# The second MLP product turned round: activations as the stationary operand, weights as 512 moving columns

## The chip, the cores and the metric

The kernel runs on one core of one Trainium2 chip. The metric is the device time of one execution in microseconds (us). The kernel before is given by the median of three runs; the profile is of one further execution.

## What is computed

One decoder layer with a convolution mixer, for 256 tokens (`T`) and 2048 channels (`D`), all in 32-bit floats. Cut to what matters:

```
mod = silu(c) @ mod_w + mod_b                  # six rows of 2048: sh1 sc1 g1 sh2 sc2 g2
h = rms_norm(x) * (1 + sc1) + sh1
y = conv_mixer(h)                              # product 2048 -> 4096, gate, causal conv, layer norm, product 2048 -> 2048
x = x + (1 + g1) * y
h = rms_norm(x) * (1 + sc2) + sh2
u = square(relu(h @ mlp_w1))                   # 2048 -> 8192
x = x + (1 + g2) * (u @ mlp_w2)                # 8192 -> 2048: the second MLP product
```

## The kernel before

**Layout.** Activations lie by channels: a tile is 128 channels by 256 tokens, and the residual `xs` is [128, 16, 256], 16 such tiles. All products before the change take a 128x128 block of weights as the stationary operand of TensorE and stream tokens as moving columns.

**Splitting into two parts.** A float is split into a high part in a shorter format (float32r) and a low part, the rest. `split_w` does it for a weight tile (1 MB, [128, 16, 128]) in two halves: ScalarE writes `hi` (L200), VectorE writes `lo` (L201, by subtraction; on GpSimd for a few tiles). There are six `hi` and six `lo` buffers of half a tile. `split_act` does the same for activations: the tile has 512 columns, 256 tokens of the high part and then 256 of the low part (ScalarE L208, VectorE L209).

**One job.** `mm` (L212 to L227) computes 128 output channels from 16 blocks of the contraction: per block one pass with `hi` stationary and all 512 columns moving (L223) and one with `lo` stationary and the 256 high columns (L224). A job does two such groups of 128 channels (c = 0, 1), into one PSUM tile `mm` of 128x2x512; there are two of these. `evac` adds the two halves: ScalarE copies one (L423), VectorE adds (L424). The out stage and the very last job use the `merged` form, three passes of 256 columns into the same columns (L219 to L221).

**Jobs in a row.** `jobs` lists 16 "in" jobs, 8 "out" jobs, and then for each of four quarters of the 8192 hidden channels 8 jobs ("up", q, i) and 8 jobs ("down", q, i). An up job ends with relu, square and `split_act` into `u2[i]`; a down job reads `u2` and adds its result, times the gate column of g2, into `xs` (L891). In the last quarter each down job sends its part of `xs` to the output (L895).

**Loads.** Every weight tile comes by one DMA of 1 MB on SyncE's queue (`top_up`, L180) into one of five `raw` buffers, in the order of the list `order`: for each job the two tiles of the next job, then the tiles named in `after[job]`. A load waits in the queue until its buffer is free.

**The modulation.** Rows of `mod` that are needed late are computed beside the jobs. The 16 tiles of g2 are "columns": `mod_col` multiplies a 1 MB tile of `mod_w` by a broadcast of silu(c) (`cb`) on VectorE with a running sum (L299), which yields one column of 128 values. `LATE_UP` and `LATE_DOWN` say how many of the 16 follow each job of the first quarter; `after[job]` holds them.

**Order on the engines.** A scheduler sets each engine's order once, at build time, from priorities and its own estimate of durations. `urgent()` raises a priority, `tc.issue_after` pins one instruction behind another. At run time an engine takes its instructions strictly in that order.

Of the kernel before, what the change touches and what calls it, by code (L numbers as in the profile page):

```python
# [14 lines left out]
P = 128  # L15
# [41 lines left out]
K_OUTER = [("out", 0), ("up", 0, 1), ("up", 0, 2)]  # L57
SIDE = 14
POOLED = [("out", 0), ("out", 1), ("up", 0, 1), ("up", 0, 2)]
LATE_UP = [0, 0, 1, 1, 1, 1, 2, 2]  # L60
LATE_DOWN = [1] * 8


@with_exitstack
def conv_block(ctx: ExitStack, tc: tile.TileContext, x, vec, dwq, c_row, mod_r, mod_c, w_first, w_in, w_out, w1, w2, out):
# [2 lines left out]
    const = ctx.enter_context(tc.tile_pool(name="const", bufs=1))  # L68
    wts = ctx.enter_context(tc.tile_pool(name="wts", bufs=1))
    acts = ctx.enter_context(tc.tile_pool(name="acts", bufs=1))  # L70
    tmp = ctx.enter_context(tc.tile_pool(name="tmp", bufs=2))
    ps = ctx.enter_context(tc.tile_pool(name="ps", bufs=2, space=PSUM))

# [62 lines left out]
    def source(key):  # L136
        kind = key[0]
        if kind == "mod":
            return mod_r[ROWS.index(key[1]), key[2]]
        if kind == "col":  # L140
            return mod_c[COLS.index(key[1])]
        if kind == "first":
            return w_first[key[1]]
        if kind == "in":
            return w_in[key[1] + key[2] * KT]
        if kind == "out":
            return w_out[2 * key[1] + key[2]]
        if kind == "up":
            return w1[key[1] * KT + 2 * key[2] + key[3]]
        if kind == "down":  # L150
            return w2[2 * key[2] + key[3], key[1]]
        if kind == "x":
            return x
        return vec[:, soon:]
# [56 lines left out]
    def mm(p, c, key, acts_of, ks=range(KT), merged=False):  # L211
        halves = parts[key]  # L212
        for k in ks:
            hi, lo = halves[k // HALF]
            m = acts_of[k // 2][:, k % 2, :]
            if merged:
                out_p, begin, end = p[:, c, 0:T], k == 0, k == KT - 1
                w = hi[:, k % HALF, :]
                nc.tensor.matmul(out_p, w, m[:, 0:T], start=begin, stop=False)  # L219
                nc.tensor.matmul(out_p, w, m[:, T : 2 * T], start=False, stop=False)  # L220
                state["mm_end"] = nc.tensor.matmul(out_p, lo[:, k % HALF, :], m[:, 0:T], start=False, stop=end)  # L221
                continue
            nc.tensor.matmul(p[:, c, :], hi[:, k % HALF, :], m, start=(k == 0), stop=(k == KT - 1))  # L223
            state["mm_end"] = nc.tensor.matmul(  # L224
                p[:, c, T : 2 * T], lo[:, k % HALF, :], m[:, 0:T], start=False, stop=(k == KT - 1),
                skip_group_check=True,
            )  # L227

    row_ps = []
    pending = []  # L230
# [153 lines left out]
    for job in jobs:  # L384
        n = quota.get(job, 0)
        after[job], late = late[:n], late[n:]
        if job[0] in ("up", "down") and job[1] == 0:
            n = (LATE_UP if job[0] == "up" else LATE_DOWN)[job[2]]
            after[job], last = last[:n], last[n:]
    assert not late and not last  # L390

# [315 lines left out]
    for n, job in enumerate(jobs):  # L707
# [8 lines left out]
        if n == KT - 1:  # L716
            for key in parts_early:
                split_w(key, nc.gpsimd)
        p = ps.tile([P, 2, 2 * T], F32, name="mm", bufs=2)
        kind, i = job[0], job[-1]  # L720
        plain = kind == "up" and job[1] == 0 and i < UNSCALED
        if job == ("up", 0, 0):
            mm(p, 0, job + (0,), xa, range(SIDE))
            for at in range(2 * UNSCALED):
                shift_row(at, shown.pop(("up", 0, at // 2, at % 2)))
            fold_shift()
            mm(p, 0, job + (0,), xa, range(SIDE, KT))
            mm(p, 1, job + (1,), xa)
        elif job in K_OUTER:
            for k2 in range(HALF):  # L730
                for c in range(2):
                    mm(p, c, job + (c,), xa if plain else hl, range(2 * k2, 2 * k2 + 2), kind == "out")
        elif kind == "in":
            rows = list(after[job]) if i < KT - 1 else []
            for c in range(2) if i < KT - 1 else (1, 0):
                for ks in (range(HALF), range(HALF, KT)):
                    mm(p, c, job + (c,), hl, ks, i == KT - 1)
                    with tc.issue_after(state["mm_end"].ins):
                        mods(rows[:1])
                    del rows[:1]  # L740
        else:
            for c in range(2):
                mm(p, c, job + (c,), u2 if kind == "down" else hl, merged=kind == "out" or n == len(jobs) - 1)
        mod_finish()
        if kind == "in":
            with urgent():
# [118 lines left out]
        elif kind == "up":  # L865
            if job[1:] == (0, 0):
                for k2 in range(HALF):
                    modulate(k2, scaled(k2, r2), SH2, SC2, ps_two())
            with urgent() if plain else ExitStack():
                t2 = evac(p)  # L870
                a = two()
                if plain:
                    nc.vector.tensor_tensor(t2, t2, spread(r2), op=ALU.mult)
                    for c in range(2):
                        at = 2 * i + c
                        nc.scalar.activation(t2[:, c, :], t2[:, c, :], AF.Relu, bias=shc[:, at : at + 1])
                    nc.vector.tensor_tensor(a, t2, t2, op=ALU.mult)
                else:
                    nc.scalar.activation(t2, t2, AF.Relu)
                    nc.scalar.activation(a, t2, AF.Square)  # L880
            u2[i] = mp.tile([P, 2, 2 * T], F32R, name="u2", bufs=HALF)
            split_act(u2[i], a)
            mods(after[job])
        else:
            mods(after[job])
            halves = [slice(0, 1), slice(1, 2)] if n == len(jobs) - 1 else [slice(0, 2)]
            for cs in halves:
                t2 = evac(p, cs) if n < len(jobs) - 1 else p[:, cs, 0:T]
                for c in range(cs.start, cs.stop):
                    xk = pair_of(xs, i)[:, c, :]  # L890
                    nc.vector.scalar_tensor_tensor(  # L891
                        xk, t2[:, c - cs.start, :], mcol(G2, 2 * i + c), xk, op0=ALU.mult, op1=ALU.add
                    )
# [54 lines left out]
```

## Time and profile before

| what | value |
|---|---|
| median of 3 runs | 1124.28 us (1123.37 to 1127.79) |
| profiled execution, its own time | 1122.33 us |
| span of the profiled execution | 1120.5 us |
| TensorE busy | 98% of the span |
| VectorE, ScalarE, GpSimd busy | 69%, 52%, 15% |
| mean granted TensorE clock | 0.997 |
| data read from HBM | 290.14 MB, 261 GB/s over the span |

The profile is of one core. Times are in us from the span's start; "mean" columns and pieces marked so are in ns. A busy share is an average over stages. In the timeline a line gives the start, the duration, engine, source line and operation with "output<-inputs" and, in brackets, how long the engine was idle before and what ended that. Matmuls are pipelined: the distance from start to start, not the duration shown, is what one costs in a stream.

### The profile page before, as it was taken

To read this page: it belongs to the slowest core of one execution; us is meant where nothing else is said; L and a number is where in the kernel's file an instruction comes from. 1 tells how busy PE (TensorE), PEld (TensorE's weight loads), DVE (VectorE), ACT (ScalarE), POOL (GpSimd) and SP (SyncE) were. 2 spreads that over 40 slices of the span, in tenths; PEclk is the share of its full clock that TensorE was granted. 3 is DMA by queue.
4 is the path that set the end of the run, shared out by engine and by line. 5 is a ranking of instruction groups with operands and counts; after the bars stand their busy time and mean duration, and the time that the engine had idled before them with its cause. 6 is when DMAs were issued, how large, how long until landed. Compare 5 with 4: busy or idle time off the path is not lost.

```text
span 1120.5 us, 17425 instructions
## 1 busy us (share of the span) xinstructions
PE 1098.4 (98%) x7088; PEld 946.6 (84%) x7088; DVE 768.0 (69%) x1025; ACT 582.0 (52%) x806; POOL 166.6 (15%) x103
## 2 busy tenths in 40 slices
PE   6999999999999999999999999999999999999998
PEld 4888776766699998888888888888888888888888
DVE  3988689987489989887765555555555665555653
ACT  5222395664675587554445554444655444555441
POOL 0000086467533262000000000000000000000000
PEclk8999999999999999999999999999999999999999
DMA  9999979888599977888775555555554655555640
GB/s 384 420 421 420 418 307 346 349 322 318 207 390 350 371 283 276 290 350 299 273 259 192 190 193 194 193 191 193 189 190 165 211 188 188 188 188 188 209 139 29
DMA packets 41553, 293.35 MB, mean 262 GB/s; under 512 B 4609, under 2 KB 5121, under 8 KB 6401
## 3 DMA queue, kind: packets, MB, share of 16 engines
q1 hardware_dynamic: 41328, 292.17, 70.4%
q8 instruction: 55, 0.90, 0.3%
q14 instruction: 24, 0.20, 0.0%
q10 hardware_dynamic: 146, 0.08, 0.0%
HBM read 290.14 MB, written 2.10 MB: 261 GB/s over the span
## 4 chain that ended last, share of the span: by engine, by line
PE 86%; DMA 6%; DVE 6%; ACT 1%; issue 0%; POOL 0%; DVEq 0%; ACTq 0%; POOLq 0%
PE mm L223 45%; PE mm L224 24%; DMA raw<-mod_c 4%; PE mm L220 3%; DVE raw L299 3%; PE mm L219 3%; PE mm L221 3%; PE row L241 2%; PE mm L669 2%; DMA raw<-w_in 1%; PE small L319 1%; DVE lo L470 1%; PE mm L111 1%; PE mm L486 1%; PE acc L669 0%
## 5 line engine op out<-in xcount | busy, mean ns | idle before, releaser
L200 ACT ACTIVATE hi<-raw 128x1024 fp32r<-128x1024 f32 x320 | 335.3, 1057 | 355.9 <-PE mm L223 327.1
L201 DVE TENSOR_TENSOR lo<-raw,hi 128x1024 fp32r<-128x1024 f32 x272 | 333.6, 1232 | 234.4 <-ACT hi L200 233.4
L223 PE MATMUL mm<-hl,hi 128*128 128x512 f32 x1184 | 414.3, 393 | 0.4 <-DVE u L686 0.4
L223 PE MATMUL mm<-u,hi 128*128 128x512 f32 x1056 | 366.8, 390 | 0.0
L224 PE MATMUL mm<-hl,lo 128*128 128x256 f32 x1184 | 332.2, 281 | 0.0
L224 PE MATMUL mm<-u,lo 128*128 128x256 f32 x1056 | 297.7, 282 | 0.0
L223 PEld LDWEIGHTS mm<-hl,hi 128*128 128x128 f32 x1184 | 221.6, 187 | 58.2 <-issue 8.4
L223 PEld LDWEIGHTS mm<-u,hi 128*128 128x128 f32 x1056 | 198.2, 188 | 41.7 <-DVE small L332 0.2
L224 PEld LDWEIGHTS mm<-hl,lo 128*128 128x128 f32 x1184 | 223.7, 189 | 5.1 <-issue 4.2
L224 PEld LDWEIGHTS mm<-u,lo 128*128 128x128 f32 x1056 | 199.6, 189 | 0.1
L299 DVE SCALAR_TENSOR_TENSOR raw<-raw,cond 128x2048 f32<-128x2048 f32 x64 | 148.3, 2320 | 20.3 <-DMA raw<-mod_c 14.7
L201 POOL TENSOR_TENSOR lo<-raw,hi 128x1024 fp32r<-128x1024 f32 x48 | 118.1, 2482 | 198.0 <-ACT hi L200 198.0
L561 DVE SCALAR_TENSOR_TENSOR acc<-u,v,acc 128x256 f32<-128x256 f32 x224 | 94.7, 490 | 1.9
L220 PE MATMUL mm<-hl,hi 128*128 128x256 f32 x288 | 81.5, 284 | 0.8 <-DVE hl L209 0.8
L219 PE MATMUL mm<-hl,hi 128*128 128x256 f32 x288 | 80.5, 284 | 1.2 <-ACT hl L208 0.8
L221 PE MATMUL mm<-hl,lo 128*128 128x256 f32 x288 | 81.1, 283 | 0.0
L219 PEld LDWEIGHTS mm<-hl,hi 128*128 128x128 f32 x288 | 54.6, 192 | 2.8 <-ACT hl L208 1.7
L220 PEld LDWEIGHTS mm<-hl,hi 128*128 128x128 f32 x288 | 55.2, 192 | 1.6 <-DVE hl L209 1.2
L221 PEld LDWEIGHTS mm<-hl,lo 128*128 128x128 f32 x288 | 55.2, 192 | 0.0
L646 ACT ACTIVATE wide<-u 32x284 f32<-32x284 f32 x110 | 48.2, 438 | 2.7 <-DVE u L686 1.4
L423 ACT ACTIVATE two<-mm 128x512 f32<-128x512 f32 x70 | 40.9, 584 | 13.5 <-PE mm L224 13.5
L523 ACT ACTIVATE two<-two,modc,amp 128x256 f32<-128x256 f32 x16 | 9.6, 599 | 71.2 <-DVE modc L279 71.2
(166 smaller groups left out, 916.7 us busy)
## 6 DMA issues: line engine op xcount, KB each, us to landing
raw<-w SPq DMA_DIRECT2D x128, 1024.0 KB, 4.9
raw<-mod_c SPq DMA_DIRECT2D x64, 1024.0 KB, 10.8
raw<-mod_r SPq DMA_DIRECT2D x32, 1024.0 KB, 7.9
raw<-w_in SPq DMA_DIRECT2D x16, 1024.0 KB, 7.2
raw<-w_out SPq DMA_DIRECT2D x16, 1024.0 KB, 7.4
first<-w_first SPq DMA_DIRECT2D x15, 1024.0 KB, 16.1
x<-x SPq DMA_DIRECT2D x2, 1024.0 KB, 6.9
x<-x SPq DMA_DIRECT2D x1, 2048.0 KB, 9.8
```

The source lines that it names most:

```text
L200: nc.scalar.activation(hi, w[:, ks, :], AF.Copy)
L201: end = engine.tensor_tensor(lo, w[:, ks, :], hi.bitcast(F32), op=ALU.subtract)
L219: nc.tensor.matmul(out_p, w, m[:, 0:T], start=begin, stop=False)
L220: nc.tensor.matmul(out_p, w, m[:, T : 2 * T], start=False, stop=False)
L221: state["mm_end"] = nc.tensor.matmul(out_p, lo[:, k % HALF, :], m[:, 0:T], start=False, stop=end)
L223: nc.tensor.matmul(p[:, c, :], hi[:, k % HALF, :], m, start=(k == 0), stop=(k == KT - 1))
L224: state["mm_end"] = nc.tensor.matmul(p[:, c, T : 2 * T], lo[:, k % HALF, :], m[:, 0:T], start=False, stop=(k == KT - 1), skip_group_check= ...
L241: state["row_end"] = nc.tensor.matmul(row_ps[0][32 * k : 32 * k + 32, :], cz[:, 4 * kg + k, 3 - b : 35 - b], w[:, 4 * k : 4 * k + 4, :], s ...
L299: nc.vector.scalar_tensor_tensor(w, w, 1.0, cb, op0=ALU.mult, op1=ALU.mult, accum_out=acc)
L423: nc.scalar.activation(t1, p[:, cs, T : 2 * T], AF.Copy)
L561: nc.vector.scalar_tensor_tensor(out, s, w, acc, op0=ALU.mult, op1=ALU.add)
L646: nc.scalar.activation(dst, src, AF.Copy)
```

## The change

The four second products ("down") are turned round. A pair of jobs ("down", q, 2j) and ("down", q, 2j+1) now makes 512 output channels for all 256 tokens: a 128x128 block of `u2` (channels by tokens) is stationary, and 512 columns of weights, four 128-column blocks of the `hi` or `lo` tile, are moving. Each pair of jobs uses both PSUM halves of one `mm` tile, one for each 128 tokens, and job 2j covers the first 8 blocks of the contraction, 2j+1 the other 8. The weight tensor is laid out on the host to suit; a load is still 1 MB.

The result then lies by tokens, so three more things are done. The residual has to lie by tokens: after job ("up", 0, 3) `turn` transposes it in 32x32 blocks on VectorE (eight instructions) and writes it to a DRAM tile, and after ("up", 0, 6) `fetch` reads it back with the blocks in their places, over the same SBUF tile. The gate g2 has to be a row: after ("up", 0, 7) `gate_row` writes the 16 columns to DRAM as one row and reads it back broadcast to all partitions, into `cb`. And all 16 columns of g2 must be known by then: `LATE_UP` takes all of them, and `LATE_DOWN` is gone. A pair of jobs is evacuated by a product with the gate row and an addition on VectorE; ScalarE's copy is gone. In the last job the second token half is cut into two pieces of 256 columns.

```diff
-LATE_UP = [0, 0, 1, 1, 1, 1, 2, 2]
-LATE_DOWN = [1] * 8
+LATE_UP = [0, 0, 2, 2, 3, 3, 3, 3]
+TURN_AT = 3
+FETCH_AT = 6
...
+    def mm_tokens(p, job):
+        last = job[1:] == (QUARTERS - 1, HALF - 1)
+        steps = [(k, t, slice(0, 512)) for k in range(HALF) for t in range(2)]
+        if last:
+            parts_of = [(0, slice(0, 512)), (1, slice(0, T)), (1, slice(T, 2 * T))]
+            steps = [(k, t, cs) for t, cs in parts_of for k in range(HALF)]
+        for k, t, cs in steps:
+            hi, lo = [w[:, 4 * (k % 2) : 4 * (k % 2) + 4, :].rearrange("p k n -> p (k n)")[:, cs]
+                      for w in parts[job + (k // 4,)][k // 2 % 2]]
+            at = HALF * (job[2] % 2) + k
+            m = u2[at // 2][:, at % 2, :]
+            begin, end = at == 0, at == KT - 1
+            p_hi, p_lo = [m[:, n : n + P] for n in (t * P, T + t * P)]
+            nc.tensor.matmul(p[:, t, cs], p_hi, hi, start=begin, stop=False, skip_group_check=True)
+            nc.tensor.matmul(p[:, t, cs], p_hi, lo, start=False, stop=False, skip_group_check=True)
+            nc.tensor.matmul(p[:, t, cs], p_lo, hi, start=False, stop=end, skip_group_check=True)
+
+    def turn(xs):
+        for k2 in range(HALF):
+            b = two()
+            nc.vector.transpose(b.rearrange("p a t -> p (a t)"), pair_of(xs, k2).rearrange("p a t -> p (a t)"))
+            nc.sync.dma_start(turned[2 * k2 : 2 * k2 + 2].rearrange("k p t -> p k t"), b)
+
+    def fetch(xs):
+        xt = xs.rearrange("p k t -> p (k t)").rearrange("p (b f) -> p b f", b=2)
+        for b in range(8):
+            nc.sync.dma_start(
+                xt[32 * (b % 4) : 32 * (b % 4) + 32, b // 4, :].rearrange("p (a t) -> p a t", t=32),
+                turned[:, :, 32 * b : 32 * b + 32].rearrange("k (a p) t -> p (k a) t", p=32),
+            )
+        return xt
+
+    def gate_row():
+        nc.sync.dma_start(gates[0].rearrange("(k p) -> p k", p=P), modc[:, G2 * KT : G2 * KT + KT])
+        nc.sync.dma_start(cb, gates.to_broadcast([P, D]))
...
-        p = ps.tile([P, 2, 2 * T], F32, name="mm", bufs=2)
         kind, i = job[0], job[-1]
+        if kind != "down" or i % 2 == 0:
+            p = ps.tile([P, 2, 2 * T], F32, name="mm", bufs=2)
...
+        elif kind == "down":
+            mm_tokens(p, job)
         else:
             for c in range(2):
-                mm(p, c, job + (c,), u2 if kind == "down" else hl, merged=kind == "out" or n == len(jobs) - 1)
+                mm(p, c, job + (c,), hl, merged=kind == "out")
...
-        else:
-            mods(after[job])
-            halves = [slice(0, 1), slice(1, 2)] if n == len(jobs) - 1 else [slice(0, 2)]
-            for cs in halves:
-                t2 = evac(p, cs) if n < len(jobs) - 1 else p[:, cs, 0:T]
-                for c in range(cs.start, cs.stop):
-                    xk = pair_of(xs, i)[:, c, :]
-                    nc.vector.scalar_tensor_tensor(
-                        xk, t2[:, c - cs.start, :], mcol(G2, 2 * i + c), xk, op0=ALU.mult, op1=ALU.add
-                    )
+            if job == ("up", 0, TURN_AT):
+                turned = scratch.tile([KT, P, T], F32, name="turned")
+                turn(xs)
+            if job == ("up", 0, FETCH_AT):
+                xt = fetch(xs)
+            if job == ("up", 0, HALF - 1):
+                gates = scratch.tile([1, D], F32, name="gates")
+                gate_row()
+        elif i % 2:
+            at = 512 * (i // 2)
+            last = n == len(jobs) - 1
+            for t, cs in [(0, slice(0, 512))] + ([(1, slice(0, T)), (1, slice(T, 2 * T))] if last else [(1, slice(0, 512))]):
+                y = two().rearrange("p a t -> p (a t)")[:, cs]
+                os = slice(at + cs.start, at + cs.stop)
+                nc.vector.tensor_tensor(y, p[:, t, cs], cb[:, os], op=ALU.mult)
+                nc.vector.tensor_tensor(xt[:, t, os], xt[:, t, os], y, op=ALU.add)
                 if job[1] == QUARTERS - 1:
-                    nc.sync.dma_start(out[:, 2 * i + cs.start : 2 * i + cs.stop, :], pair_of(xs, i)[:, cs, :])
+                    nc.sync.dma_start(out[:, t, os], xt[:, t, os])
```

More of the change, by code (lines that the diff above doesn't have):

```diff
@@ L386, in conv_block @@
         after[job], late = late[:n], late[n:]
-        if job[0] in ("up", "down") and job[1] == 0:
-            n = (LATE_UP if job[0] == "up" else LATE_DOWN)[job[2]]
+        if job[:2] == ("up", 0):
+            n = LATE_UP[job[2]]
             after[job], last = last[:n], last[n:]
@@ L924 @@
     w_first = np.ascontiguousarray(w_in[tiles].transpose(2, 1, 0, 3))
+    w2 = np.asarray(mlp_w2)[0].reshape(QUARTERS, 2, 2, 4, P, 4, 512).transpose(0, 5, 1, 2, 4, 3, 6)
+    w2 = np.ascontiguousarray(w2.reshape(QUARTERS, KT // 2, 2, P, KT, P))
     arrays = {
@@ L937 @@
         "w1": blocks(np.asarray(mlp_w1)[0])[:, 0],
-        "w2": blocks(np.asarray(mlp_w2)[0]),
+        "w2": w2,
     }
@@ L946 @@
     y = r.results[0]["out"]
-    return np.ascontiguousarray(y.transpose(1, 0, 2).reshape(D, T).T)[None]
+    return np.ascontiguousarray(y.transpose(1, 0, 2).reshape(T, D))[None]
```

5 lines of the change are left out of this document (3 added, 2 removed).

## The prediction

> **What bounds the kernel now.** I read the page first (span, busy time, the chain that ended last), then the windows of the MLP, then TensorE's timeline inside them.
>
> ```profile
> span 1120.5 us, 17425 instructions
> PE 1098.4 (98%) x7088; PEld 946.6 (84%) x7088; DVE 768.0 (69%) x1025; ACT 582.0 (52%) x806; POOL 166.6 (15%) x103
> PE 86%; DMA 6%; DVE 6%; ACT 1%; issue 0%; POOL 0%; DVEq 0%; ACTq 0%; POOLq 0%
> ...
> core 0: us, PE busy (x) PEld busy (x) DVE busy (x) ACT busy (x) POOL busy (x), PEclk, DMA share, GB/s
> 410.00:500.00 90.00, 90.00 (x543) 79.40 (x533) 76.31 (x90) 60.99 (x88) 13.80 (x6) 1.00 0.85 310
> 500.00:587.00 87.00, 87.00 (x504) 77.11 (x503) 65.35 (x76) 38.16 (x43) 0.00 (x0) 1.00 0.77 282
> 587.00:675.00 88.00, 88.00 (x509) 77.63 (x508) 49.01 (x48) 49.43 (x61) 0.00 (x0) 1.00 0.56 191
> ```
>
> TensorE is busy in every microsecond of these windows at a granted clock of 1.00, and the chain is 86% TensorE. So an edit gains only by shortening TensorE's own stream, and loses as soon as anything makes TensorE wait. The window 410 to 500 is the first up quarter: VectorE has 13.7 us idle of 90 and DMA runs at a share of 0.85, by far the tightest stretch of the MLP. The change loads exactly this stretch.
>
> Below, u0 to u7 are the jobs ("up", 0, i) and d0 to d7 the jobs ("down", 0, i). Starts on TensorE:
>
> ```profile
> 439.76 0.39 PE L223 MATMUL mm<-hl,hi 128*128 128x512 f32 x1
> 473.04 0.39 PE L223 MATMUL mm<-hl,hi 128*128 128x512 f32 x1
> 506.33 0.39 PE L223 MATMUL mm<-u,hi 128*128 128x512 f32 x1
> ...
> 700.13 0.39 PE L223 MATMUL mm<-u,hi 128*128 128x512 f32 x1
> 700.36 0.28 PE L224 MATMUL mm<-u,lo 128*128 128x256 f32 x1
> 700.48 0.39 PE L223 MATMUL mm<-u,hi 128*128 128x512 f32 x1
> ...
> 350.03 0.28 PE L219 MATMUL mm<-hl,hi 128*128 128x256 f32 x1
> 370.19 0.28 PE L219 MATMUL mm<-hl,hi 128*128 128x256 f32 x1
> ...
> 1109.61 0.28 PE L219 MATMUL mm<-u,hi 128*128 128x256 f32 x1
> 1116.49 0.28 PE L221 MATMUL mm<-u,lo 128*128 128x256 f32 x1
> ...
> 134.06 3.45 PE mm L486 x16
> ```
>
> 439.76, 473.04 and 506.33 are the starts of u3, u6 and d1. From u3 to d1 six jobs take 66.57 us, 11.095 each without a gap; a job is 32 pairs of a 512- and a 256-column pass, so a pair takes 346.7 ns. Inside a pair (700.13 to 700.48) the 512 pass takes about 230 and the 256 pass 117 to 120.
>
> **Passes of the down jobs.** Before, a job is 32x512 + 32x256 = 24,576 columns in 64 passes; after, 8 k by 2 token halves by 3 passes of 512 columns: 48 passes, again 24,576 columns. The matrix work is the same; only a fixed cost per pass can go. A 256 pass alone takes 120.0 ns in the out stage (350.03 to 370.19, 168 passes) and 116.7 in the last job (1109.61 to 1116.49, 59 steps). Subtracted from the pair, a 512 pass costs 226.7 or 230.0; I take the middle, 228.3. Then a new job is 48 x 0.2283 = 10.96 us, 0.135 less than 11.095. It counts for 30 jobs (d0 ends in a wait, below; the last job is apart): -4.0 us. Ends: 230.0 gives -1.7, 226.7 gives -6.4. The farthest row is L486, another data type, at 3.45/16 = 216 ns per record of the same length: 10.37 per job, -21.8 us.
>
> The Trainium skill, page "TensorE: Matmul & The Clock Gate", section "Back-to-back issue gap", gives N/2.4 + 2.5 ns per isolated pass: 216 for 512 and 109 for 256. A pair would then take 325 ns; this trace shows 346.7, so the rule does not hold here for the old stream. If it holds for 512-only streams, the L486 end above comes true; that is a rival below.
>
> **Evacuation and tail.** The old down jobs' evacuation (ScalarE copy, VectorE add, two multiply-adds) becomes two products and two adds per pair of jobs; VectorE has 39 of 88 us idle in 587 to 675, so that counts as nothing, and would cost a few tenths of a us per pair if uncovered. The last job does.
>
> ```profile
> 1116.81 0.88 DVE L891 SCALAR_TENSOR_TENSOR x<-mm,modc,x 128x256 f32<-128x256 f32 x2 [8.96 <-PE mm L221]
> out<-x SPq DMA_DIRECT2D x2, 128.0 KB, 1.7
> ...
> L424 DVE TENSOR_TENSOR two<-mm,two 128x512 f32<-128x512 f32 x63 | 43.1, 684 | 4.0 <-ACT two L423 4.0
> L514 DVE TENSOR_TENSOR two<-x,r 128x512 f32<-128x512 f32 x8 | 5.5, 686 | 0.0
> L877 DVE TENSOR_TENSOR two<-two 128x512 f32<-128x512 f32 x2 | 3.1, 1528 | 0.0
> ```
>
> Both old halves wait for the very last matmul (8.96 idle, then 0.88 of work). In the new program, too, the last job's only signal from TensorE stands on its last matmul, so all three pieces follow it: products and adds of 512, 256 and 256 columns, about 0.60 + 2x0.41 twice, 2.8 us. That is +2.0; the last DMA has the same 128 KB. The last job's passes: 24 x 228.3 + 48 x 116.7 = 11.08 against 96 x 116.7 = 11.20, -0.1.
>
> **VectorE in the first up quarter.** Eight column products of G2 (L299) move from d0-d7 into u2-u7, and eight transposes of a 128x512 tile are added.
>
> ```profile
> L200 ACT ACTIVATE hi<-raw 128x1024 fp32r<-128x1024 f32 x320 | 335.3, 1057 | 355.9 <-PE mm L223 327.1
> ...
> 446.44 2.29 DVE L299 SCALAR_TENSOR_TENSOR raw<-raw,cond 128x2048 f32<-128x2048 f32 x1
> 448.64 0.09 DVE L299 DVE_READ_ACCUMULATOR raw<-raw,cond 128x1 f32 x1
> 448.64 0.69 DVE L209 TENSOR_TENSOR u<-two,u 128x512 fp32r<-128x512 f32 x1
> 449.25 1.22 DVE L201 TENSOR_TENSOR lo<-raw,hi 128x1024 fp32r<-128x1024 f32 x1
> 450.39 0.15 DVE L279 TENSOR_TENSOR modc<-modc,v 128x1 f32<-128x1 f32 x1
> 450.46 1.22 DVE L201 TENSOR_TENSOR lo<-raw,hi 128x1024 fp32r<-128x1024 f32 x1
> ```
>
> Back to back a column product holds VectorE 2.29 us, a weight half's low part (lo) 1.14, a 512-column operation 0.61, a bias 0.07. No row shows a transpose: L514, one pass over 128x512, says 0.6; the dearest row of that shape, L877, says 1.5. I take 0.6. Added: 8 x 2.29 + 8 x 0.61 = 23.2 us, against 13.7 idle. VectorE falls behind by about 9.5 us.
>
> Where that hurts follows from the order in which the changed program's instructions stand on VectorE (an order, without times). In the old run the low part of u2's activations starts at 448.64; in the new order one more column product and one more lo stand ahead of it: about 452.1. From there to u4's evacuation stand six column products (13.7), eight lo (9.1), eight transposes (4.9), u3's evacuation and the low parts of u2 and u3 (1.8) and biases (0.3): 29.8. So u4 is evacuated at 482 to 482.6. There are two "mm" PSUM tiles, and u6 takes u4's: TensorE, due at 473.04, waits about 9.5 us. That is the first new wait. It delays the end only as far as the second one does not swallow it.
>
> **The turned residual in the DMA queue.** SyncE's queue is in order, and each weight load in it waits for its buffer.
>
> ```profile
> SPq L180 <- DVE lo L201: 535.6, 118, 7.2
> ...
> raw<-w SPq DMA_DIRECT2D x128, 1024.0 KB, 4.9
> ...
> 5.30:8.90 3.60, 3.60 (x6) 1.26 (x4) 0.00 (x0) 2.19 (x4) 0.00 (x0) 1.00 1.02 422
> 1118.10:1119.20 1.10, 0.00 (x0) 0.00 (x0) 0.00 (x0) 0.00 (x0) 0.00 (x0) 1.00 0.68 238
> ```
>
> The first row is the rule of that queue: 535.6 us spent waiting for lo to free a buffer. The 8 writes of `turn` are 2,048 rows of 1 KB. The 8 reads of `fetch` are the novelty: each is 32 partitions by 64 runs of 32 floats, 2,048 runs of 128 bytes, 16,384 in all, 1,024 per DMA engine. No row shows such runs. The window at 1118 holds the two last output transfers, 256 rows of 1 KB: 1.10 x 16 x 0.68 / 256 = 46.8 ns per row and engine. At 5.30 to 8.90 rows of 8 KB move at 422 GB/s, 317 ns each. The line through both gives 13.0 ns at 128 bytes: 13.3 us for the fetch. The price of a 1 KB row for each gives 47.9. The line leaves out the gaps between packets, and the last 128 KB output, 8 rows per engine or 0.37 us, took 1.7 from issue to landing; so I take the geometric middle, X = 25 us, and keep 13 and 48.
>
> The Trainium skill, page "DMA: Bandwidth & Descriptors", section "Why small descriptors are slow (HBM only)", counts 3 cycles beside one per 32 bytes, so 7 cycles for 128 bytes; at the 850 MHz of its section "Where 436 GB/s comes from" the fetch is an estimated 8.4 us. With that the forecast would be some 17 us lower; no run here shows it.
>
> The new order on SyncE is: d0's second weight tile, a column, four fetches, a column, a fetch, a column, three fetches, and only then d1's first weight tile. d0's second tile waits for the last lo of u7. On VectorE four lo, three column products, u5's evacuation and two low parts stand between u4's evacuation and that: 4.6 + 6.9 + 1.8 = 13.3, so it is issued at about 495.8. Five tiles of 1 MB at 422 GB/s take 12.4 us, the fetch X, the landing 2.4 (4.9 less 2.5), hi and lo 2.2: d1 starts at 512.8 + X, where it stood at 506.33. The two waits together cost 6.5 + X = 31.5 us. d0 ends near 504.3 + 11 = 515, so the second wait shows on TensorE as X - 2.5.
>
> The `gate_row` writes 2,048 runs of 4 bytes (128 per engine, at most 128 x 46.8 ns = 6 us) and the 1 MB broadcast follow; behind them on SyncE wait loads for d3 and later, with a job of 11 us or more to spare, and the first reader is the evacuation after d1. Counted at nothing, 6 us if that cover is gone. Removed ScalarE copies lie off the path.
>
> **Sum.** Against the profiled execution's own 1122.33 us (span 1120.5 and 1.8 around it): -4.0 - 0.1 + 2.0 + 31.5 = +29.4, 1151.7. The median of the runs is 1.95 above that execution, so I forecast 1154.
>
> **Rivals.**
> 1. Faster. The 512 stream runs at L486's 216 ns, and the fetch is nearly hidden because the queue gets to it earlier than VectorE's backlog says. Place: 30 down jobs, -21.8. For: the pass pitch is the one thing TensorE must gain from, and 48 fixed costs replace 64. Against: pair and single pitch agree on 227 to 230. It beats the old kernel by over 0.5% only if both waits together stay under 14 us; with none of them left it gives 1104. Chance 0.12.
> 2. No change. The pitch is 228, and VectorE catches up, say because a transpose is cheaper and the loads lie ahead: 2 us of waits left, 1124. Against: 23.2 us into 13.7 idle. Chance 0.10.
> 3. Pitch 216 with the waits as worked out: 1136. Chance 0.15.
> 4. Each 128-byte run costs as much as a 1 KB row or more: 1177 and up. Chance 0.15.
> 5. My forecast, X between 13 and 40: 1142 to 1169. Chance 0.48.
>
> **Range and chances.** About 0.5% is what a measurement of this kernel can tell from no change, 5.6 us. Faster 0.12 (rival 1), same 0.10 (rival 2), slower 0.78 (3, 4 and the forecast). The low end joins pitch 216 and X = 13 and reaches a little into rival 2: 1122. The high end is X = 48 with dear transposes (8 x 0.9 more): 1184. The forecast's own range is 1142 to 1169.
>
> **What would show it.** Right: TensorE idle near 473 before the first matmul of u6, ended by VectorE's evacuation or its followers; a longer idle before d1, ended by hi or lo of a tile that lay behind the fetch; after that down jobs of 10.9 to 11.0 us without gaps; 2.8 us of VectorE after the last matmul. The fetch shows as a stretch with DMA busy but few GB/s. Wrong: no idle TensorE around d1, or down jobs of 10.4 us, or waits that come back in every quarter.

## The result and the profile after

| | before | after |
|---|---|---|
| median | 1125.64 us (1123.37 to 1127.79, 4 runs) | 1153.85 us (1151.52 to 1157.00, 4 runs) |
| profiled execution: its time, its span | 1122.33 us, 1120.5 us | 1157.00 us, 1155.2 us |

The changed kernel takes 1.0253 times as long, with a 95% interval of 1.0219 to 1.0287: 28 us more.

First the page of the changed kernel (span, busy time, the chain that ended last), then its windows: the same three stretches as before, and three short ones in the first quarter.

```profile
span 1155.2 us, 16314 instructions
PE 1113.1 (96%) x6568; PEld 926.6 (80%) x6568; DVE 766.0 (66%) x1004; ACT 566.6 (49%) x775; POOL 166.4 (14%) x103
PE 81%; DVE 9%; DMA 8%; issue 1%; ACT 0%; DVEq 0%; SPq 0%; ACTq 0%
...
core 0: us, PE busy (x) PEld busy (x) DVE busy (x) ACT busy (x) POOL busy (x), PEclk, DMA share, GB/s
410.00:500.00 90.00, 79.49 (x550) 69.56 (x549) 81.09 (x103) 53.34 (x82) 19.37 (x8) 0.92 0.90 339
500.00:587.00 87.00, 81.07 (x357) 65.52 (x356) 49.29 (x52) 34.73 (x37) 0.00 (x0) 0.96 0.84 265
587.00:675.00 88.00, 88.00 (x468) 74.81 (x467) 49.99 (x50) 43.82 (x51) 0.00 (x0) 1.00 0.55 190
...
490.00:495.00 5.00, 5.00 (x21) 4.25 (x21) 5.00 (x7) 2.96 (x4) 0.00 (x0) 0.65 1.02 409
505.00:510.00 5.00, 5.00 (x31) 4.43 (x30) 4.28 (x4) 2.95 (x4) 0.00 (x0) 1.00 0.99 157
530.00:535.00 5.00, 4.54 (x12) 3.42 (x12) 4.68 (x5) 3.97 (x5) 0.00 (x0) 0.56 1.02 428
```

TensorE, which had been busy through all of 410 to 587, now misses 10.5 us in the first window and 5.9 in the second, and its mean clock falls to 0.92 and 0.96. From 587 on it is gapless again. The window at 505 is the sign that the prediction named for the fetch: the DMA engines are full (0.99) but move only 157 GB/s. At 490 and 530 TensorE works at a clock of 0.65 and 0.56.

TensorE's timeline of the changed kernel at the two waits (L225 and L226 are the old L223 and L224; L244 to L246 are the three passes of `mm_tokens`):

```profile
477.07 0.28 PE L226 MATMUL mm<-hl,lo 128*128 128x256 f32 x1
487.72 0.77 PE L225 MATMUL mm<-hl,hi 128*128 128x512 f32 x1 [10.36 <-DVE modc L317]
...
523.59 0.40 PE L246 MATMUL mm<-hi,u 128*128 128x512 f32 x1
529.45 0.80 PE L244 MATMUL mm<-hi,u 128*128 128x512 f32 x1 [5.47 <-ACT hi L202]
530.71 0.79 PE L245 MATMUL mm<-lo,u 128*128 128x512 f32 x1 [0.46 <-DVE lo L203]
```

The first wait stands ahead of u6, the second ahead of d1. What ended them stands on VectorE (L462 is the evacuation of u4; L203 the low part of a weight half) and ScalarE (L461 a copy for the evacuation, L202 the high part):

```profile
486.92 0.65 DVE L462 TENSOR_TENSOR two<-mm,two 128x512 f32<-128x512 f32 x1
529.43 2.36 DVE L203 TENSOR_TENSOR lo<-raw,hi 128x1024 fp32r<-128x1024 f32 x2 [7.59 <-ACT hi L202]
...
481.58 0.60 ACT L461 ACTIVATE two<-mm 128x512 f32<-128x512 f32 x1 [7.97 <-DMA turned<-two]
528.34 2.00 ACT L202 ACTIVATE hi<-raw 128x1024 fp32r<-128x1024 f32 x2 [12.20 <-DMA raw<-w]
```

The bracket at u6 names the tiny bias L317 that VectorE did last; the event that mattered is the evacuation just ahead of it. ScalarE's copy for that evacuation had waited for a buffer that a write of `turn` still held, but it was done at 482.2, 4.7 us before VectorE came to it: VectorE is busy in every microsecond from 450 to 488, so its backlog set the time. At d1 the chain goes lo, hi, and a weight tile's DMA.

SyncE's queue before d1 (L182 are loads, L257 the fetch):

```profile
490.00 3.81 SPq L182 DMA_DIRECT2D raw<-w  x2
496.35 0.33 SPq L182 DMA_DIRECT2D raw<-mod_c  x1
497.46 10.33 SPq L257 DMA_DIRECT2D x<-turned  x4
507.84 1.88 SPq L182 DMA_DIRECT2D raw<-mod_c  x1
509.77 0.43 SPq L257 DMA_DIRECT2D x<-turned  x1
510.30 4.24 SPq L182 DMA_DIRECT2D raw<-mod_c  x1
514.59 5.90 SPq L257 DMA_DIRECT2D x<-turned  x3
520.59 4.67 SPq L182 DMA_DIRECT2D raw<-w  x5
```

The eight reads are issued from 497.46 on; d1's first tile is issued only behind them, at 520.59. In the trace's packets the fetch is 16,384 of 128 bytes, 13.0 ns each, 13.35 us of the 16 engines.

To see where the rest of the time is, the starts of the quarters on TensorE were read off in each trace. The table gives the length of each stretch: u2 to u7 of the first up quarter, then the down (D) and up (U) quarters in order.

| us | start of u2 | u2-u7 | D0 | U1 | D1 | U2 | D2 | U3 | D3 | after the last matmul |
|---|---|---|---|---|---|---|---|---|---|---|
| before | 428.66 | 66.57 | 88.75 | 88.75 | 88.75 | 88.75 | 88.75 | 88.75 | 88.74 | 4.05 |
| after | 432.39 | 80.24 | 98.02 | 90.45 | 89.61 | 88.75 | 89.60 | 90.45 | 89.57 | 6.14 |

Four of the starts of the changed kernel:

```profile
610.65 0.39 PE L225 MATMUL mm<-hl,hi 128*128 128x512 f32 x1
701.10 0.40 PE L244 MATMUL mm<-hi,u 128*128 128x512 f32 x1
790.71 0.40 PE L225 MATMUL mm<-hl,hi 128*128 128x512 f32 x1
879.46 0.40 PE L244 MATMUL mm<-hi,u 128*128 128x512 f32 x1
```

610.65 to 701.10 is the second up quarter, 90.45 us for 256 pairs, 353.3 ns each; 790.71 to 879.46 is the third, 88.75 us and 346.7 ns, with the same instructions. Neither has a gap.

The differences of the columns add up to the 34.7 us between the two spans: 3.7 before u2, 13.7 and 9.3 in the first two stretches, 1.7 in U1 and in U3, 0.85 in each of D1 to D3, 2.1 at the end. The first 3.7 arise where both programs are the same. In other runs of the same front part (below) u2 starts anywhere from 428.4 to 431.8, in two variants of the changed kernel at 428.9, so they belong to the execution and not to the change; without them the difference is 31.0.

### The profile page after: what moved, and what is told of

Same layout as the page of the kernel before. It is cut to its first block, busy times and chain, and to the rows that moved or that the text cites. A ratio compares the mean times of both kernels' runs of the same rounds, so it can differ in the third digit from the quotient of the medians.

```text
span 1155.2 us, 16314 instructions
## 1 busy us (share of the span) xinstructions
PE 1113.1 (96%) x6568; PEld 926.6 (80%) x6568; DVE 766.0 (66%) x1004; ACT 566.6 (49%) x775; POOL 166.4 (14%) x103
## 4 chain that ended last, share of the span: by engine, by line
PE 81%; DVE 9%; DMA 8%; issue 1%; ACT 0%; DVEq 0%; SPq 0%; ACTq 0%
PE mm L225 23%; PE mm L226 11%; PE mm L245 10%; PE mm L246 10%; PE mm L244 10%; DMA raw<-mod_c 7%; DVE raw L337 5%; PE mm L222 3%; PE mm L221 3%; PE mm L223 3%; PE row L279 2%; PE mm L707 2%; DVE lo L203 1%; PE small L357 1%; DVE lo L508 1%
## 5 line engine op out<-in xcount | busy, mean ns | idle before, releaser
L202 ACT ACTIVATE hi<-raw 128x1024 fp32r<-128x1024 f32 x320 | 334.4, 1057 | 376.4 <-PE mm L246 194.1
L203 DVE TENSOR_TENSOR lo<-raw,hi 128x1024 fp32r<-128x1024 f32 x272 | 334.0, 1235 | 256.5 <-ACT hi L202 256.1
L225 PE MATMUL mm<-hl,hi 128*128 128x512 f32 x1184 | 420.7, 399 | 10.5 <-DVE modc L317 10.4
L226 PE MATMUL mm<-hl,lo 128*128 128x256 f32 x1184 | 333.1, 281 | 0.0
L225 PEld LDWEIGHTS mm<-hl,hi 128*128 128x128 f32 x1184 | 223.4, 189 | 73.0 <-issue 19.4
L226 PEld LDWEIGHTS mm<-hl,lo 128*128 128x128 f32 x1184 | 224.6, 190 | 5.2 <-issue 4.2
L244 PE MATMUL mm<-hi,u 128*128 128x512 f32 (+1 forms) x520 | 204.8, 394 | 5.5 <-ACT hi L202 5.5
L245 PE MATMUL mm<-lo,u 128*128 128x512 f32 (+1 forms) x520 | 204.7, 394 | 0.5 <-DVE lo L203 0.5
L246 PE MATMUL mm<-hi,u 128*128 128x512 f32 (+1 forms) x520 | 204.5, 393 | 0.0
L203 POOL TENSOR_TENSOR lo<-raw,hi 128x1024 fp32r<-128x1024 f32 x48 | 117.8, 2477 | 199.1 <-ACT hi L202 199.1
L244 PEld LDWEIGHTS mm<-hi,u 128*128 128x128 f32 x520 | 98.2, 189 | 28.8 <-ACT hi L202 5.9
L245 PEld LDWEIGHTS mm<-lo,u 128*128 128x128 f32 x520 | 98.2, 189 | 23.7 <-DVE lo L203 1.0
L246 PEld LDWEIGHTS mm<-hi,u 128*128 128x128 f32 x520 | 98.2, 189 | 23.2
L222 PE MATMUL mm<-hl,hi 128*128 128x256 f32 x288 | 82.9, 289 | 2.0 <-DVE hl L211 2.0
L221 PE MATMUL mm<-hl,hi 128*128 128x256 f32 x288 | 81.6, 288 | 1.2 <-ACT hl L210 0.8
L223 PE MATMUL mm<-hl,lo 128*128 128x256 f32 x288 | 82.5, 288 | 0.0
L222 PEld LDWEIGHTS mm<-hl,hi 128*128 128x128 f32 x288 | 56.4, 196 | 2.8 <-DVE hl L211 2.4
L221 PEld LDWEIGHTS mm<-hl,hi 128*128 128x128 f32 x288 | 55.9, 196 | 2.7 <-ACT hl L210 1.7
L223 PEld LDWEIGHTS mm<-hl,lo 128*128 128x128 f32 x288 | 56.6, 196 | 0.0
```

What stands on the lines that cost most here:

```text
L202: nc.scalar.activation(hi, w[:, ks, :], AF.Copy)
L203: end = engine.tensor_tensor(lo, w[:, ks, :], hi.bitcast(F32), op=ALU.subtract)
L226: state["mm_end"] = nc.tensor.matmul(p[:, c, T : 2 * T], lo[:, k % HALF, :], m[:, 0:T], start=False, stop=(k == KT - 1), skip_group_check= ...
L244: nc.tensor.matmul(p[:, t, cs], p_hi, hi, start=begin, stop=False, skip_group_check=True)
L245: nc.tensor.matmul(p[:, t, cs], p_hi, lo, start=False, stop=False, skip_group_check=True)
L246: nc.tensor.matmul(p[:, t, cs], p_lo, hi, start=False, stop=end, skip_group_check=True)
```

## The experiments

The theory at this point: the two waits come from VectorE's backlog (u6) and from the fetch in the DMA queue (d1), and the rest is TensorE's pace. The rivals: the waits come from the columns of g2 alone, from buffers shared with `turn`, or from late loads whatever the fetch does; and the pace comes from the orientation, from the PSUM halves, or from the length of the passes.

**The passes alone.** Token passes and their evacuation stay, `turn`, `fetch` and `gate_row` are left out, and the columns of g2 are back at their old places; the residual stays by channels.

```diff
-LATE_UP = [0, 0, 2, 2, 3, 3, 3, 3]
+LATE_UP = [0, 0, 1, 1, 1, 1, 2, 2]
+LATE_DOWN = [1] * 8
...
-            if job == ("up", 0, TURN_AT):
-                turned = scratch.tile([KT, P, T], F32, name="turned")
-                turn(xs)
-            if job == ("up", 0, FETCH_AT):
-                xt = fetch(xs)
-            if job == ("up", 0, HALF - 1):
-                gates = scratch.tile([1, D], F32, name="gates")
-                gate_row()
```

> The down jobs turned round (three 512-column passes, new evacuation and tail), but no turn, no fetch, no gate row, and the g2 columns where the old kernel had them; residual and gate are taken unturned, so the output is not the reference's. Theory from the changed kernel's trace: a 512-column pass costs 233 ns in a 512-only stream, a down job 11.20 us instead of 11.09 (31 jobs: +3.3), tail +2.0, no wait: about +5 us against before. Rival, the prediction's own step: 228.3 ns a pass, 10.96 a job, -4 and +2.0: about -2 us. To see besides: whether up jobs of 11.30 us (quarters 2 and 4 of the changed kernel) come back here.

Measured: 1131.98 us, 1.0059 times the kernel before (1.0039 to 1.0079). u2-u7 66.57, D0 to D3 89.59, 89.61, 89.60, 89.57, U1 and U3 90.45, U2 88.75, 5.99 at the end. There is no wait. So turning the product costs about 7 us by itself, where the prediction had it at 2 us less (-4.1 of passes, +2.0 of tail); and the slower up quarters come with it, which no theory had.

**The columns alone.** The kernel before, with all 16 columns of g2 in the first up quarter.

```diff
-LATE_UP = [0, 0, 1, 1, 1, 1, 2, 2]
-LATE_DOWN = [1] * 8
+LATE_UP = [0, 0, 2, 2, 3, 3, 3, 3]
+LATE_DOWN = [0] * 8
```

> The old kernel with nothing changed but the place of the g2 columns: all sixteen in the first up quarter. Theory A (the first wait is the transposes': their buffers and their share of VectorE): 18.3 us of column products into 13.7 idle leave VectorE a few us late, but the evacuations stand early in its order, so TensorE waits 0 to 2 us. Rival B (VectorE's backlog from the columns is enough): TensorE waits about 5 us around u6 and runs at half clock behind it, +5 to +8 us.

Measured: 1128.90 us, 1.0045 (1.0025 to 1.0065). TensorE does not wait at u6. It waits in d0, where the old order needs u7's activations at its fifteenth block. TensorE's timeline of this kernel there:

```profile
502.99 0.28 PE L224 MATMUL mm<-u,lo 128*128 128x256 f32 x1
506.70 0.79 PE L223 MATMUL mm<-u,hi 128*128 128x512 f32 x1 [3.43 <-DVE u L209]
507.29 0.41 PE L224 MATMUL mm<-u,lo 128*128 128x256 f32 x1
...
507.93 0.41 PE L224 MATMUL mm<-u,lo 128*128 128x256 f32 x1
```

D0 takes 95.07 us instead of 88.75: 3.6 of waiting, and then some nine pairs at 640 ns (507.29 to 507.93) instead of 347. Columns without transposes make VectorE late, but not by enough for u6; the eight transposes are needed for that.

**The fetch in long rows.** The eight reads as rows of 8 KB, without putting the blocks in their places.

```diff
-                xt[32 * (b % 4) : 32 * (b % 4) + 32, b // 4, :].rearrange("p (a t) -> p a t", t=32),
-                turned[:, :, 32 * b : 32 * b + 32].rearrange("k (a p) t -> p (k a) t", p=32),
+                xt[32 * (b % 4) : 32 * (b % 4) + 32, b // 4, :],
+                turned[2 * b : 2 * b + 2].rearrange("k (p a) t -> (k p) (a t)", a=8),
```

> The changed kernel, with the eight reads of fetch as 8 KB rows of the same 2 MB (the residual lands in a wrong arrangement). Theory: the 16,384 runs of 128 bytes took 13.0 ns each, 13.4 us; as 8 KB rows they take 5.0, so the second wait (5.9 and 1.5 in pieces, and some 2 at half clock) loses 8.4 and nearly goes: -7 to -9 us against the changed kernel. Rival (the second wait is the queue's order and VectorE's lag, whatever the run length): -1 to 0. The first wait, about 10.6, stays in both.

Measured: 1150.03 us, 1.0216 (1.0184 to 1.0248): u2-u7 80.92 and D0 97.99, the same two waits. The median is 3.8 us below the changed kernel's, between the two expectations, and these two stretches did not get shorter. This run doesn't tell the theories apart. The scheduler put the reads elsewhere in the queue, from 476.92 on, and over 470 to 530 a row of 8 KB took 391 ns on average against 336 in the changed kernel. The 16 engines have no time left in that stretch of 60 us in either kernel (61.5 us of packets here, 59.8 there). Why the rows were dearer here is not shown.

**Buffers of their own for `turn`.**

```diff
-            b = two()
+            b = mp.tile([P, 2, T], F32, name="flip", bufs=2)
```

> The changed kernel, with two buffers of their own for the eight transposes instead of the shared six named two, which the evacuations use as well. In the order on VectorE the transposes then stand in the out stage, and u4's evacuation ahead of four of the six column products. Theory (the copy of u4's PSUM tile waited 8.0 us for a buffer that a turned write held): no wait at u6, 10.6 and 2.7 at half clock come back, fetch stands earlier in the queue, so the second wait goes too: -15 to -22 us against the changed kernel. Rival (VectorE's work in the up quarter is too much wherever the transposes stand): 18.3 us of columns into 13.7 idle, a wait of 5 us or more stays: -5 to -10.

Measured: 1142.08 us, 1.0151 (1.0120 to 1.0181), 12 us less than the changed kernel, between the two expectations. But more than the buffers changed: with them the scheduler put all transposes into the out stage and the fetch at about 418. The wait at u6 is gone (u2-u7 68.36); small waits stand in the out stage, ahead of d0 and in D0, of which the timeline of TensorE shows three:

```profile
391.68 0.39 PE L221 MATMUL mm<-hl,hi 128*128 128x256 f32 x1 [2.17 <-ACT hi L202]
...
393.84 0.58 PE L223 MATMUL mm<-hl,lo 128*128 128x256 f32 x1 [1.66 <-DVE lo L203]
...
503.32 0.49 PE L244 MATMUL mm<-hi,u 128*128 128x512 f32 x1 [1.63 <-ACT hi L202]
```

So most of the two waits is a matter of where the transposes and the fetch stand. That the shared buffers themselves cost anything at their old place is not shown.

**Without the fetch.** The changed kernel without the eight reads; the residual stays unturned.

```diff
-        for b in range(8):
-            nc.sync.dma_start(
-                xt[32 * (b % 4) : 32 * (b % 4) + 32, b // 4, :].rearrange("p (a t) -> p a t", t=32),
-                turned[:, :, 32 * b : 32 * b + 32].rearrange("k (a p) t -> p (k a) t", p=32),
-            )
```

> The changed kernel without the eight reads of the fetch; the transposes and their writes stay, and the residual is left unturned. If the reads themselves delay d1 (13.35 us of packets on engines that are busy anyway), the wait at u6 stays at about 10.6 us, the one before d1 and its slow passes go (7.7 us of waiting, about 1.5 of half clock): D0 falls from 98.0 to about 89, the time to about 1145. If the loads are late only because VectorE frees their buffers late, D0 stays at 98 and the time at 1154.

Measured: 1144.41 us, 1.0180 (1.0158 to 1.0201), 9.4 us less than the changed kernel. u2-u7 77.91, D0 89.59: the wait at u6 is still 9.4 us, the one at d1 and the slow passes behind it are gone. The queue of this kernel (L182 are loads):

```profile
494.17 4.88 SPq L182 DMA_DIRECT2D raw<-mod_c  x3
502.58 11.31 SPq L182 DMA_DIRECT2D raw<-w  x5
```

d1's first tile is issued at 502.58 instead of 520.59. This settles the second wait: the reads make it. They take 13.35 us of the engines, and without them D0 is 8.4 us shorter, all that it had lost to waiting and to the slow passes. Whether it is the time of their packets or that of their issue (one read held the queue for 7.2 us) that keeps d1's load back, no run separates.

**A wider second pass in the old orientation.** The kernel before; in the down jobs the pass with `lo` stationary moves all 512 columns, which adds one product more than wanted.

```diff
+            wide = key[0] == "down"
...
-                p[:, c, T : 2 * T], lo[:, k % HALF, :], m[:, 0:T], start=False, stop=(k == KT - 1),
+                p[:, c, :] if wide else p[:, c, T : 2 * T], lo[:, k % HALF, :], m if wide else m[:, 0:T],
```

> The kernel before, with the second pass of each pair in the down jobs widened from 256 to all 512 moving columns (one product more than wanted is added): a stream of 512-column passes alone in the old orientation, 64 a job. If a stream of 512-column passes alone runs at 233.3 ns whatever is stationary, a down job takes 14.93 us, 3.84 more than 11.09, for 31 jobs +119: about 1244; the up quarters 2 and 4 should then also show 11.30 us a job. If 233.3 belongs to the new orientation and these run at 226.7 to 230, a job takes 14.5 to 14.7 us, +106 to +113: 1231 to 1238, and all up quarters stay at 11.09.

Measured: 1248.91 us, 1.1110 (1.1089 to 1.1132). D0 to D2 take 119.47, 119.46 and 119.46 us, 512 passes each, and all of U1, U2 and U3 90.45. The passes in TensorE's timeline of this kernel:

```profile
539.73 0.39 PE L225 MATMUL mm<-u,lo 128*128 128x512 f32 x1
...
540.66 0.39 PE L225 MATMUL mm<-u,lo 128*128 128x512 f32 x1
```

Four passes in 0.93 us, 233.3 ns by the length of the quarter. So the pace of the new down jobs comes with passes of 512 columns alone and not with the orientation.

**One PSUM half after the other.** The passes alone, with all passes of the first 128 tokens of a job ahead of those of the second.

```diff
-        steps = [(k, t, slice(0, 512)) for k in range(HALF) for t in range(2)]
+        steps = [(k, t, slice(0, 512)) for t in range(2) for k in range(HALF)]
```

> The run with the token passes alone (no turned residual, no gate row, the g2 columns at their old places; 1131.98 us), in which each job now makes all passes of the first 128 tokens before those of the second, so that the PSUM half changes once in 24 passes and not after every third. If the change of the PSUM half costs the 5 ns over 228.3 in a pass, a down job falls from 11.20 to about 10.96 us and the time by 31 x 0.24 = 7 us to about 1125, or by 11 if the up quarters 2 and 4 also come back to 11.09. If not, 1132 and 233.3 ns.

Measured: 1131.13 us, 1.0075 (1.0050 to 1.0100), every stretch as with the passes alone (D0 89.59, U1 90.45). The change of the PSUM half costs nothing.

**TensorE kept busy in the waits.** The changed kernel with spare passes ahead of u6 and d1.

```diff
+        if job in (("up", 0, 6), ("down", 0, 1)):
+            spare = ps.tile([P, 512], F32, name="row", bufs=1)
+            for _ in range(40 if kind == "up" else 22):
+                with tc.issue_after(state["mm_end"].ins):
+                    state["mm_end"] = nc.tensor.matmul(spare, hl[0][:, 0, 0:P], hl[0][:, 0, :], start=True, stop=True)
```

> The changed kernel with 40 spare 512-column passes put ahead of u6's matmuls and 22 ahead of d1's, into a PSUM tile that nobody reads. They fill about 9 of the 10.6 us of the first wait and 5 of the 5.9 of the second. If the slow pairs behind each wait (about nine pairs at 641 ns instead of 347) come from TensorE having been idle, they go: 2.7 us at u6 and about 1.5 at d1, so about 1150. If the lower clock comes from something else (the full DMA queue, say), the spare passes change nothing, 1154, or add what sticks out of the waits, up to 1156.

Measured: 1153.43 us, 1.0270 (1.0241 to 1.0298), no less than the changed kernel. TensorE's timeline of this kernel at both places (L765 are the spare passes):

```profile
481.70 0.84 PE L765 MATMUL row<-hl 128*128 128x512 f32 x3
482.59 0.47 PE L225 MATMUL mm<-hl,hi 128*128 128x512 f32 x1
...
520.15 1.07 PE L765 MATMUL row<-hl 128*128 128x512 f32 x4
525.01 0.50 PE L244 MATMUL mm<-hi,u 128*128 128x512 f32 x1 [3.80 <-ACT hi L202]
...
526.87 0.63 PE L246 MATMUL mm<-hi,u 128*128 128x512 f32 x1
527.29 0.63 PE L244 MATMUL mm<-hi,u 128*128 128x512 f32 x1
```

At u6 the slow pairs are gone, so the lower clock does come from TensorE's idling, even with the DMA queue full. u2-u7 takes 75.97 us instead of 80.24: 2.7 us of slow pairs, and u6 also starts 1.6 us earlier after u2. But D0 takes 101.12 instead of 98.02. From the start of u2 to that of d1 it is 96.1 us here and 97.1 in the changed kernel: the loads set when d1 starts, so what is saved at u6 is waited for at d1. At d1 the spare passes ran out 3.8 us too early, and the passes behind the wait are slow again (427 ns).

**Spare passes that shift the start of each job.** The passes alone, and the kernel before, with one short pass ahead of each job, 32 columns for the first job of a quarter to 256 for the eighth. (In the down quarters of the second kernel the one of 64 columns stands 28 passes into its job.)

```diff
+        if kind == "down" or (kind == "up" and job[1] > 0):
+            spare = ps.tile([P, 512], F32, name="row", bufs=1)
+            cols = 32 * (i + 1)
+            with tc.issue_after(state["mm_end"].ins):
+                state["mm_end"] = nc.tensor.matmul(spare[:, 0:cols], hl[0][:, 0, 0:P], hl[0][:, 0, 0:cols], start=True, stop=True)
```

On the passes alone:

> The run with the token passes alone (1131.98 us) with one spare pass ahead of each job of the down quarters and of up quarters 2 to 4, into a PSUM tile that nobody reads: 32 columns ahead of the first job of a quarter, 32 more ahead of each next one, 256 ahead of the eighth. Their own cost is about 8 x (32 to 256 columns, 20 to 120 ns), 0.5 us a quarter. If the two paces (226.7 or 233.3 ns for a 512-column pass, a pair at 346.7 or 353.3) depend on when a stream starts, jobs within one quarter now differ: 11.09 beside 11.30 in up quarters, and 10.9 beside 11.20 in down quarters. If a pace belongs to the stream itself, every down job stays at 11.20, and the time is 1132 + 3.5 = 1135.

On the kernel before:

> The kernel before with the same spare passes. If the pace depends on when a stream starts, some jobs go from 11.09 to 11.30 us (a pair from 346.7 to 353.3 ns), up to +0.21 each, and the time to 1128 to 1138. If the slower pace comes only behind a stream of 512-column passes, all jobs stay at 11.09 and the time is 1124 + 3.5 = 1127.5.

Measured: 1138.14 us (1.0123, 1.0094 to 1.0153) and 1135.79 us (1.0094, 1.0068 to 1.0120). The up quarters take 91.13 us in both. In the kernel before, whose up quarters had all been at the faster pace, seven of the eight jobs of each are now at the slower one. The starts of jobs 3 to 5 of U1 in TensorE's timeline of that kernel, and of jobs 4 and 5 of D1:

```profile
610.51 0.46 PE L223 MATMUL mm<-hl,hi 128*128 128x512 f32 x1
...
621.74 0.45 PE L223 MATMUL mm<-hl,hi 128*128 128x512 f32 x1
...
633.17 0.44 PE L223 MATMUL mm<-hl,hi 128*128 128x512 f32 x1
...
712.46 0.45 PE L223 MATMUL mm<-u,hi 128*128 128x512 f32 x1
...
723.70 0.43 PE L223 MATMUL mm<-u,hi 128*128 128x512 f32 x1
```

Less the spare pass ahead of the next job, 0.06 to 0.08 us, the two up jobs are 11.16 and 11.36: only the job behind 96 columns is fast, and the same one in every up quarter of both kernels. So what stands ahead of a stream of 512 and 256 columns can set its pace, and the stream keeps it. But that isn't all: the down job behind 128 columns, the same kind of stream behind the same spare pass, takes 11.16 us where the up job takes 11.36, and no down job of this kernel goes to the slower pace. Down jobs of 512 columns alone take 11.19 to 11.28 us whatever stands ahead of them (11.20 plus the first pass's start): there no faster pace was found.

## Why the prediction was right, and where it was not

The total of +29.4 came out as +28.2 between the medians, and the direction came from the two waits, as forecast. Below the total, terms missed in both directions, and that they nearly cancelled was luck. The terms as predicted, and as read off the profiled execution:

| term | forecast | measured |
|---|---|---|
| passes of the down jobs, last job included | -4.1 | +3.3 (D0 from d1 on 0.7, then 0.83 to 0.86 a quarter) |
| up quarters | 0 | +3.4 (U1 and U3) |
| start of d1, by both waits | 6.5 + X = +31.5 | +19.4 |
| slow passes behind the second wait (0.5 of it idle for lo) | 0 | +2.8 |
| after the last matmul | +2.0 | +2.1 |
| sum | +29.4 | +31.0, and 3.7 ahead of the change |

**The passes (wrong).** The step that failed takes a pass's cost from the mixed stream by subtraction, 228.3 ns, and hands it to a stream of 512 alone. There it is 233.3, and the down jobs of 10.9 to 11.0 us that the prediction named as its sign did not come. TensorE's timeline of the changed kernel in the second down quarter, three passes apart:

```profile
749.64 0.40 PE L245 MATMUL mm<-lo,u 128*128 128x512 f32 x1
...
750.34 0.40 PE L245 MATMUL mm<-lo,u 128*128 128x512 f32 x1
```

That is 700 ns for three, and 48 x 233.3 = 11.20 us a job instead of 10.96. The wider passes in the old orientation show that this belongs to the length of the passes. Rivals 1 and 3, with 216 ns, are out. Nor was the row that they went by a pass of the same length, as the prediction has it; in the kernel before, its passes move 256 columns:

```profile
L486 PE MATMUL mm<-two,first 128*128 128x256 f32 x160 | 36.2, 379 | 0.0
```

The 216 ns that the Trainium skill's page "TensorE: Matmul & The Clock Gate", section "Back-to-back issue gap", gives for 512 columns does not hold for these streams either. Fewer, longer passes gain nothing on this kernel: 48 of 512 cost more than 32 of 512 and 32 of 256, at the same number of columns.

**The up quarters (not foreseen).** The prediction counted only the jobs that it changed. U1 and U3 lost 1.7 us each with the same instructions. The spare passes show that what stands ahead of a stream can change its pace, but the down jobs show that it is not the only thing; what makes the two paces stays open.

**The first wait (right).** u4's evacuation was forecast at 482 to 482.6, on the old clock of the span; with the 3.7 us of later start that is 485.7 to 486.3, and it came at 486.92. The wait was forecast at 9.5 us and was 10.5. The transposes, priced at 0.6 from L514, took 0.59 to 0.63 us from start to start.

**The second wait (right in kind, X too large).** Place, order and releasers are as predicted, and the run without the fetch shows the reads to be the cause. The mis-sized term is X: 25 us, the middle between 13.3 and 47.9, where the packets took 13.35. The line through the two rows, 13.0 ns for 128 bytes, was exact; the argument for going above it (gaps between packets) failed: while the reads' packets ran, from 501.5 to 523.3, the engines' share was 0.97, with other packets between them. The 8.4 us that the prediction estimated by the Trainium skill's page "DMA: Bandwidth & Descriptors", section "Why small descriptors are slow (HBM only)", are too low here. As a delay of d1's load X is more than its packets: counted from the start of u2, that load is issued 17.4 us later than in the run without the fetch. With X = 13.35 the formula gives 19.85 for d1's delay; it was 19.4. Part of that is luck: the load ahead of the fetch was issued before 493.81 instead of at 499.5 (495.8 and the later start), and the way from there to d1 took 36 us instead of 30.

**The slow passes (not foreseen).** Behind each wait TensorE ran at half clock, 427 ns a pass, for 5.7 us at u6 and 5.0 at d1. At u6 that cost 2.7 us that the second wait swallowed, as the run with spare passes shows; at d1 another 2.8, with the 0.5 idle for lo, that nothing swallowed. Had this been in the sum, X at the packets' 13.35 would have given -4.1 + 2.0 + 19.85 + 2.8 = +20.6, and the passes' and up quarters' +10.8 over the forecast bring it to +31.4, against the 31.0 measured. The forecast of 29.4 came out by luck: X was 11.65 too large while 13.6 us of other costs were missing.

**The tail and the gate row (right).** The last pieces on VectorE and the issue of the last transfers:

```profile
1149.07 0.28 PE L246 MATMUL mm<-hi,u 128*128 128x256 f32 x1
1149.39 1.35 DVE L939 TENSOR_TENSOR two<-mm,cond 128x512 f32<-128x512 f32 x3 [14.56 <-PE mm L246]
1150.66 1.35 DVE L940 TENSOR_TENSOR x<-x,two 128x512 f32<-128x512 f32 x3
1151.36 1.32 SPq L942 DMA_DIRECT2D out<-x  x3
```

2.6 us of VectorE behind the last matmul, forecast 2.8. VectorE once waited 3.9 us for the broadcast gate row, but no wait of TensorE came of it.

None of the kernels tried beats the one before. With `turn` in buffers of its own, 1142.08 us, the change is at its best here; what is left are the 7 us of the passes alone, and some 10 us of smaller waits and slow passes behind them (5 in the out stage, 1.8 in u2-u7, 2.9 in D0).

## What to carry to other kernels

A gapless engine only gets faster if its own stream gets shorter: time the new stream's shape before counting a gain from fewer instructions, since a pass priced inside a mixed stream needn't cost the same alone. Work that is moved into the tightest stretch has to be added up on every engine and every queue there, and of two waits in a row only the one that sets the next start counts. Where terms are uncertain, a right total is no proof of the terms: read each off the trace.

## What the runs showed of the hardware

- With the columns alone, a wait of 3.6 us was enough for half clock (pairs at 640 instead of 347 ns behind it). With own buffers, two waits of 2.17 and 1.66 us in the out stage, with two passes between them, were enough too (256-column passes at 213 instead of 120 ns behind them); one of 1.63 us ahead of d0 was not (clock 1.00 over D0). Full clock came back 3.2 to 6.1 us after the first pass behind a wait. The Trainium skill's page "TensorE: Matmul & The Clock Gate", section "What's actually happening", puts an idle window at about 3.4 us and the release after as long a busy one, and has these windows run free of the kernel. By that the release would come one to two windows after the first pass, an estimate of 3.4 to 6.8 us, and the runs agree but for a little. The two short waits show that the stretch ahead of half clock need not be free of passes.
- A 512-column pass of this data type took 228 to 232 ns on average in one pace and 236 to 237 in the other when 256-column passes stood between (a pair 346.7 or 353.3), and 233.3 in a stream of its own, in either orientation.
- A 128-byte packet from DRAM took 13.0 ns of a DMA engine in the changed kernel's full queue (13.6 in the run with spare passes at the waits), and the 1 KB rows of `turn` 46.1 ns.
